# A decoder block on one core: x tile 0 by halves on a second queue, and the first head's q projected between V's k-tiles

## The chip, the core and the metric

The kernel runs on one core of a Trainium2 chip. A core has five engines with a queue of instructions each: TensorE (PE in the profile), VectorE (DVE), ScalarE (ACT), GpSimd (POOL) and SyncE (SP), which here only issues transfers. They meet through semaphores. Matrix products land in eight PSUM banks. The metric is the device time of one execution in microseconds (us), lower is better.

## The reference

One layer of a decoder block on 512 tokens of width 1024, in float32:

```python
h = rmsnorm(x, norm_attn_g[l])
u = h @ w_in[l]
u_q, u_k, u_v, u_pool, u_gate = jnp.split(u, splits, axis=-1)
a = diff_attention(q, k, v, positions, lam, subln_g[l], lam_init)   # 8 heads, rotary tables from positions
p = multiscale_pool(u_pool, w_pool[l], pool_scale[l])
merged = gates[:, :, 0] * a + gates[:, :, 1] * p
x = x + (merged @ w_out[l]).astype(x.dtype)
z = jnp.square(jax.nn.relu(rmsnorm(x, norm_mlp_g[l]) @ w_up[l]))
x = x + (z @ w_down[l]).astype(x.dtype)
return rmsnorm(x, final_norm_g)
```

## The kernel before

Every product is made of three: both factors are split into a high part (`xh`, `wh`, rounded by ScalarE) and a low part (`xl`, `wl`, the difference, by VectorE), and high x high, high x low and low x high are summed in one bank.

The program begins with the V projection. x comes transposed as eight k-tiles of 128 x 512 (`gx`, issued by SyncE at L178); `xprep` turns one into `xh` (ScalarE, L179) and `xl` (VectorE, L180), `xsquare` squares it (ScalarE, L188 and L191), and GpSimd sums the squares into `ssx` (L192). x has four buffers, so tile k+4 is fetched when tile k has been used. V has two halves of 512 columns (the loop over `n`, L203). In each, four banks take the four token tiles, and for each k-tile there are twelve matmuls of 512 columns (L221 to L223). V's weights come in tiles of two k-tiles, by halves in the first half; `split_w` casts a half (ScalarE, L112) and subtracts (VectorE, L113).

Behind V's first half `pr` (bank 4, L228) and `pc` (bank 5, L233) sum `ssx` over partitions; `rsqrt` (L195 to L201) makes the reciprocal norms `rb` and `rcol` from them on ScalarE and VectorE, and V's banks are scaled by `rcol` when they are emptied (L240, L241). V's second half has banks 4 to 7, so its token tiles 0 and 1 wait until `pr` and `pc` have been read.

VectorE works out the angles of the rotary tables meanwhile (L268 to L298), ScalarE takes their sine (L299) between two table loads, and TensorE turns the tables with eight transposes (`pt`, L311). Then the heads follow: q and k of a head are projected by 24 matmuls each (`proj`, `mm3`, L127), rotated (`rope`), and the attention is computed while products of the gates and the pool fill TensorE. `wh` and `wl` have four buffers each for all weights. Banks 0 to 2 serve projections, 3 and 4 scores, 5 and 6 transposes, 7 the heads' outputs; the warm-up matmuls at the start (L165) use bank 7 too.

The order on each engine is set at build time: a scheduler takes the program's calls in their written order as priority, replays them against a model of the engines, and writes down the order that results. A call of `after` pins two instructions. So an edit early in the program changes the order of small work far behind it.

Of the kernel before, what the change touches and what calls it, by code (L numbers as in the profile page):

```python
# [18 lines left out]
P = 128  # L19
# [32 lines left out]
def block_kernel(ctx, tc, xT, x_tok, gains, pos, consts, w_in, w_v, w_pool, w_out, w_up, w_dn, out):  # L52
    nc = tc.nc
    V, A, G, T = nc.vector, nc.scalar, nc.gpsimd, nc.tensor
    EXPLN = "natural_log_exp_and_others"
    A.preload_act_table_set(EXPLN)

    def after(later, earlier):
        tc.add_manual_dep(
# [12 lines left out]
    def bank(i, name):  # L72
        return ps.tile([P, S], F32, tag=f"b{i}", name=name)
# [13 lines left out]
    def tmp(tag, name, shape=(P, S), dt=F32, bufs=2):  # L87
        return tp.tile(list(shape), dt, tag=tag, name=name, bufs=bufs)

    def f(ap):  # L90
        return ap.bitcast(F32)
# [45 lines left out]

    con = cp.tile([P, 57], F32, name="con")
    g1c, g2c, gfc, pscc = (con[:, 8 * i : 8 * i + 8] for i in range(4))
    wv0 = load_w(w_v[0, 0], "v0_0", 2, slice(0, 1))  # L140
    nc.sync.dma_start(out=g1c, in_=consts[:, 0:8])
    invc = con[:, 32:40]
    rcc = con[:, 40:56]
    subc = con[:, 56:57]
# [26 lines left out]
    rcol = cf.tile([P, NT, 2], F32, name="rcol")  # L171
    rb = cf.tile([P, S], F32, name="rb")

    gt0 = tmp("g", "gx0", (P, 4, S), bufs=1)

    def xprep(k):
        xt = gt0[:, k % 4, :]
        nc.sync.dma_start(out=xt, in_=xT[k])  # L178
        A.activation(out=xh[:, k, :], in_=xt, func=AF.Copy, scale=g1c[:, k : k + 1])  # L179
        V.scalar_tensor_tensor(  # L180
            out=xl[k], in0=xt, scalar=g1c[:, k : k + 1], in1=f(xh)[:, k, :],
            op0=ALU.mult, op1=ALU.subtract,
        )

    def xsquare(k):
        xt = gt0[:, k % 4, :]
# [8 lines left out]
    def rsqrt(dst, src, t, n):  # L195
# [4 lines left out]
        V.scalar_tensor_tensor(out=t, in0=src, scalar=n * EPS, in1=t, op0=ALU.add, op1=ALU.mult)  # L200
        V.scalar_tensor_tensor(out=dst, in0=t, scalar=-3.0, in1=dst, op0=ALU.add, op1=ALU.mult)  # L201

    for n in range(2):  # L203
        accs = [bank(4 * n + t, f"v{n}_{t}") for t in range(NT)]
        for kk in range(4):
            if n == 0:
                xprep(2 * kk)
            if n == 0 and kk == 0:
                raw, hi, lo = wv0
                nc.sync.dma_start(out=raw[:, 512:], in_=w_v[0, 0, :, 512:])  # L210
            else:
                raw, hi, lo = load_w(w_v[n, kk], f"v{n}_{kk}", 2 if n == 0 else 1)
            for k2 in range(2):
                if n == 0 and k2 == 1:
                    xprep(2 * kk + 1)
                sl = slice(k2 * 512, k2 * 512 + 512)
                split = split_w(raw, hi, lo, sl, eng=V)
                k = 2 * kk + k2
                for t in range(NT):
                    tsl = slice(t * P, t * P + P)  # L220
                    T.matmul(accs[t], lhsT=xh[:, k, tsl], rhs=hi[:, sl], start=k == 0, stop=False)  # L221
                    T.matmul(accs[t], lhsT=xh[:, k, tsl], rhs=lo[:, sl], start=False, stop=False)
                    T.matmul(accs[t], lhsT=xl[k][:, tsl], rhs=hi[:, sl], start=False, stop=k == NK - 1)  # L223
                if n == 0:
                    after(xsquare(k), split)
        if n == 0:
            pr = bank(4, "pr")
            T.matmul(pr, lhsT=ones, rhs=ssx, start=True, stop=True)  # L228
            rsqrt(rb, pr, tmp("sq", "nt1"), D)
            A.mul(out=rb, in_=rb, mul=-0.5)  # L230
            pc = bank(5, "pc")
            for t in range(NT):
                T.matmul(pc[:, 2 * t : 2 * t + 2], lhsT=ssx[:, t * P : t * P + P], rhs=ones[:, 0:2], start=True, stop=True)  # L233
            rct = cf.tile([P, NT, 2], F32, name="rct")
            rsqrt(rcol, pc[:, 0:8].rearrange("p (a b) -> p a b", a=NT), rct, D)
            A.mul(out=rcol, in_=rcol, mul=-0.5)
        for t in range(NT):
            vd = [v_[:, 4 * n : 4 * n + 4, t * P : t * P + P] for v_ in (vh, f(vh), vl)]
            av = accs[t].rearrange("p (h d) -> p h d", h=4)
            A.activation(out=vd[0], in_=av, func=AF.Copy, scale=rcol[:, t, 0:1])  # L240
            V.scalar_tensor_tensor(  # L241
                out=vd[2], in0=av, scalar=rcol[:, t, 0:1], in1=vd[1],
                op0=ALU.mult, op1=ALU.subtract,
            )
# [57 lines left out]
    for i, fill in ((0, 1.0), (1, 0.0)):  # L302
        tk = tmp("q1", f"rt{i}", (P, NT, 2, 8, 8))
        G.memset(tk, fill)
        for c in range(2):
            for x_ in range(2):
                sc = -1.0 if (i == 1 and x_ == 0) else 1.0
                V.tensor_scalar(out=tk[:, :, c, x_, :], in0=arg[:, i], scalar1=sc, scalar2=None, op0=ALU.mult)
        pt = bank((0, 1)[i], f"pt{i}")
        for t in range(NT):  # L310
            T.transpose(out=pt[:, t * P : t * P + P], in_=tk[:, t].rearrange("p c x f -> p (c x f)"), identity=ident)  # L311
        tab = cf.tile([P, S], F32, name=f"tab{i}")
        V.tensor_tensor(out=tab, in0=pt, in1=rb, op=ALU.mult)
        tabs.append(tab)
# [31 lines left out]
    def qk(h):  # L346
        qs = tp.tile([P, 2, S], F32R, tag="qs", name=f"qs{h}", bufs=2)
        ks = tp.tile([P, 2, S], F32R, tag="ks", name=f"ks{h}", bufs=2)
        kz = kzs[h % 2]
        q = rope(proj(h, f"q{h}", V), f"q{h}")  # L350
        for c, own, oth in ((0, lo_, hi_), (1, hi_, lo_)):
            A.copy(out=qs[own, c, :], in_=q[own])
            V.tensor_tensor(out=qs[oth, c, :], in0=q[own], in1=f(qs)[own, c, :], op=ALU.subtract)
# [618 lines left out]
```

## Time and profile before

| what | us |
|---|---|
| median of 3 runs | 678.95 |
| lowest and highest | 678.44, 679.31 |
| the profiled execution, its own time | 679.05 |
| its span | 677.1 |
| TensorE busy in the span | 665.5 (98%) |
| VectorE, ScalarE, GpSimd busy | 514.8, 460.8, 170.8 |
| TensorE's granted clock | 0.997 of full speed |

A busy time is the sum over an engine's instructions; which engine sets the end at a place is read from who waits there. In a row of the timeline the brackets hold the engine's idle time before the instruction and whose work ended it. Matmuls overlap, so the distance of two starts, not the duration shown, is the cost of one.

### The profile page before, as it was taken

What the parts mean: (1) busy time and instruction counts of PE and PEld (TensorE: products, weight loads), DVE (VectorE), ACT (ScalarE), POOL (GpSimd) and SP (SyncE); (2) the same over time, 40 slices, a digit from 0 to 9 for tenths busy, and PEclk for the clock granted to TensorE, in tenths of its full rate; (3) what the DMA queues carried; (4) which work ended last, traced back from release to release, by engine and by line L of the source; (5) the groups of instructions that cost most, each with busy time, mean ns of one, the idle gap of its engine ahead of it and who ended that gap; (6) DMA issues with size and microseconds to landing.
All of it is one profiled execution on the core that took longest, in us unless ns stands there. A gap on an engine that the chain in (4) does not pass through costs nothing.

```text
span 677.1 us, 10004 instructions
## 1 busy us (share of the span) xinstructions
PE 665.5 (98%) x3686; PEld 579.0 (86%) x3686; DVE 514.8 (76%) x845; ACT 460.8 (68%) x739; POOL 170.8 (25%) x169
## 2 busy tenths in 40 slices
PE   8999999999999999999999999999999999999995
PEld 7788878887888888888889988899889998899885
DVE  6953878697878966775478999667994699747995
ACT  7554577958789687985467886367743696356874
POOL 6201543255445535520201021202103021210120
PEclk9999999999999999999999999999999999999998
DMA  8624563517163455466885589676959579493963
GB/s 272 188 97 126 136 153 106 110 66 179 48 162 109 100 140 140 91 148 228 294 217 105 162 178 259 138 190 157 236 183 200 187 162 260 124 220 126 217 125 124
DMA packets 32592, 109.34 MB, mean 161 GB/s; under 512 B 4000, under 2 KB 4640, under 8 KB 32544
## 3 DMA queue, kind: packets, MB, share of 16 engines
q0 software_dynamic: 10656, 38.80, 31.9%
q1 hardware_dynamic: 21744, 69.64, 29.0%
q8 instruction: 29, 0.48, 0.3%
q10 hardware_dynamic: 144, 0.26, 0.1%
q14 instruction: 19, 0.16, 0.1%
HBM read 106.59 MB, written 2.10 MB: 161 GB/s over the span
## 4 chain that ended last, share of the span: by engine, by line
PE 77%; DVE 8%; DMA 5%; ACT 5%; issue 4%; SPq 0%; POOL 0%; DVEq 0%; ACTq 0%; POOLq 0%
PE dm L817 7%; PE dm L819 7%; PE dm L820 7%; PE um L738 7%; PE um L743 7%; PE um L740 7%; DMA wga_uNone<-w_up 4%; PE gp L131 2%; PE gp L132 2%; PE gp L135 2%; PE k L135 2%; PE k L132 2%; PE k L131 2%; PE q L131 2%; PE q L132 2%
## 5 line engine op out<-in xcount | busy, mean ns | idle before, releaser
L649 POOL DMA_DIRECT2D wga_dNone<-w_dn x16 | 14.2, 885 | 152.2 <-DVE wl_dt L113 152.2
L819 PE MATMUL dm<-wh_dt,z 128*128 128x512 f32 (+1 forms) x128 | 49.5, 386 | 0.0
L820 PE MATMUL dm<-wl_dt,z 128*128 128x512 f32 (+1 forms) x128 | 49.4, 386 | 0.0
L817 PE MATMUL dm<-wh_dt,z 128*128 128x512 f32 (+1 forms) x128 | 49.0, 387 | 0.0
L740 PE MATMUL um<-gss,wh_ut 128*128 128x256 f32 x192 | 48.1, 283 | 0.0
L738 PE MATMUL um<-gss,wh_ut 128*128 128x256 f32 x192 | 48.0, 283 | 0.0
L649 POOL DMA_DIRECT2D wga_uNone<-w_up x18 | 15.6, 865 | 118.6 <-DVE wl_ut L113 95.5
L377 ACT ACTIVATE p<-p,st 128x128 f32<-128x128 f32 (+3 forms) x64 | 35.7, 559 | 12.4 <-DVE st L373 11.8
L835 DVE TENSOR_TENSOR x<-x,dm 128x512 f32<-128x512 f32 x48 | 32.5, 679 | 15.2 <-PE dm L820 15.2
L112 ACT CAST wh_ut<-wga_uNone 128x1024 fp32r<-128x1024 f32 x24 | 24.8, 1051 | 28.1 <-PE dm L819 19.5
L112 ACT CAST wh_ub<-wr_u 128x1024 fp32r<-128x1024 f32 x24 | 25.1, 1050 | 24.0 <-PE um L740 10.9
L113 DVE TENSOR_TENSOR wl_ub<-wr_u,wh_ub 128x1024 fp32r<-128x1024 f32 x24 | 29.1, 1219 | 12.4 <-ACT wh_ub L112 12.4
L113 DVE TENSOR_TENSOR wl_ut<-wga_uNone,wh_ut 128x1024 fp32r<-128x1024 f32 x24 | 29.0, 1221 | 11.5 <-ACT wh_ut L112 11.5
L820 PE MATMUL dm<-wl_db,z 128*128 128x512 f32 x96 | 37.2, 389 | 0.0
L819 PE MATMUL dm<-wh_db,z 128*128 128x512 f32 x96 | 37.2, 389 | 0.0
L740 PEld LDWEIGHTS um<-gss,wh_ut 128*128 128x128 f32 x192 | 36.9, 192 | 0.0
L738 PEld LDWEIGHTS um<-gss,wh_ut 128*128 128x128 f32 x192 | 36.7, 192 | 0.0
L817 PE MATMUL dm<-wh_db,z 128*128 128x512 f32 x96 | 35.8, 390 | 0.0
L714 DVE TENSOR_TENSOR z<-rawz,z 128x1024 fp32r<-128x1024 f32 x28 | 33.6, 1215 | 0.5 <-ACT z L711 0.5
L112 ACT CAST wh_dt<-wga_dNone 128x1024 fp32r<-128x1024 f32 x24 | 24.7, 1047 | 13.3 <-issue 5.1
L740 PE MATMUL um<-gab,wh_ub 128*128 128x256 f32 x128 | 32.4, 284 | 0.0
L738 PE MATMUL um<-gab,wh_ub 128*128 128x256 f32 x128 | 32.1, 283 | 0.0
(316 smaller groups left out, 2246.6 us busy)
## 6 DMA issues: line engine op xcount, KB each, us to landing
wr_u<-w_up SPq DMA_DIRECT2D x24, 512.0 KB, 5.7
wr_d<-w_dn SPq DMA_DIRECT2D x24, 512.0 KB, 4.2
wga_uNone<-w_up POOLq DMA_DIRECT2D x18, 512.0 KB, 7.1
wga_dNone<-w_dn POOLq DMA_DIRECT2D x16, 512.0 KB, 5.5
wr_q<-w_in SPq DMA_DIRECT2D x8, 512.0 KB, 3.4
wr_k<-w_in SPq DMA_DIRECT2D x8, 512.0 KB, 3.8
wr_ga<-w_in SPq DMA_DIRECT2D x8, 512.0 KB, 3.3
wr_gp<-w_in SPq DMA_DIRECT2D x8, 512.0 KB, 3.4
```

What stands on the lines that cost most here:

```text
L112: ins = A.copy(out=hi[:, sl], in_=raw[:, sl])
L113: (eng or G).tensor_tensor(out=lo[:, sl], in0=raw[:, sl], in1=f(hi)[:, sl], op=ALU.subtract)
L131: T.matmul(acc, lhsT=hi[:, c], rhs=rh[:, k, :], start=k == 0, stop=False)
L132: T.matmul(acc, lhsT=hi[:, c], rhs=rl[k], start=False, stop=False)
L377: A.activation(out=pr[:, c, :N], in_=pr[:, c, :N], func=AF.Exp, scale=-1.0, bias=st[:, c : c + 1], accum_out=st[:, 2 + c : 3 + c])
L714: V.tensor_tensor(out=z[:, 1], in0=r, in1=f(z[:, 0]), op=ALU.subtract)
L738: m = T.matmul(a_, lhsT=hi[:, c], rhs=rh[:, k, :], start=p + k == 0 and onto is None, stop=False, skip_group_check=True)
L740: T.matmul(a_, lhsT=hi[:, c], rhs=rl[:, k, :], start=False, stop=False, skip_group_check=True)
L743: m = T.matmul(a_, lhsT=lo[:, c], rhs=rh[:, k, :], start=False, stop=k == 3, skip_group_check=True)
L817: m = T.matmul(a_, lhsT=zh, rhs=hi[:, sl], start=p == 0 and start, stop=False, skip_group_check=True)
L819: T.matmul(a_, lhsT=zl, rhs=hi[:, sl], start=False, stop=False, skip_group_check=True)
L820: end = T.matmul(a_, lhsT=zh, rhs=lo[:, sl], start=False, stop=p == 3, skip_group_check=True)
```

## The change

x tile 0 is fetched by two transfers of 256 columns which ScalarE issues ahead of its first table load, and is copied and subtracted by halves. SyncE sends the gain column `con` ahead of V's first weights. The weights of head 0's q are fetched and split inside V's first half (after the second weight tile), and q is projected into bank 7 in single k-tiles: the source writes those of k-tiles 0 to 3 behind V's k-tiles 4 to 7, and the other four behind V's first half, ahead of `pr`. V's second half uses banks 4, 5, 6 and 0, and the table transposes banks 3 and 2. Head 0's attention takes its q from bank 7 instead of projecting it.

```diff
-    A.preload_act_table_set(EXPLN)
...
+    gt0 = tmp("g", "gx0", (P, 4, S), bufs=1)
+    for i in range(2):
+        nc.scalar.dma_start(out=gt0[:, 0, i * 256 : i * 256 + 256], in_=xT[0, :, i * 256 : i * 256 + 256])
+    A.preload_act_table_set(EXPLN)
+    nc.sync.dma_start(out=g1c, in_=consts[:, 0:8])
     wv0 = load_w(w_v[0, 0], "v0_0", 2, slice(0, 1))
-    nc.sync.dma_start(out=g1c, in_=consts[:, 0:8])
...
     def xprep(k):
         xt = gt0[:, k % 4, :]
-        nc.sync.dma_start(out=xt, in_=xT[k])
-        A.activation(out=xh[:, k, :], in_=xt, func=AF.Copy, scale=g1c[:, k : k + 1])
-        V.scalar_tensor_tensor(
-            out=xl[k], in0=xt, scalar=g1c[:, k : k + 1], in1=f(xh)[:, k, :],
-            op0=ALU.mult, op1=ALU.subtract,
-        )
+        if k:
+            nc.sync.dma_start(out=xt, in_=xT[k])
+        for sl in (slice(0, 512),) if k else (slice(0, 256), slice(256, 512)):
+            A.activation(out=xh[:, k, sl], in_=xt[:, sl], func=AF.Copy, scale=g1c[:, k : k + 1])
+            V.scalar_tensor_tensor(
+                out=xl[k][:, sl], in0=xt[:, sl], scalar=g1c[:, k : k + 1], in1=f(xh)[:, k, sl],
+                op0=ALU.mult, op1=ALU.subtract,
+            )
...
+    def q0_step(k):
+
+        c = slice(k * P, (k + 1) * P)
+        hi, lo = wq0[1:]
+        T.matmul(q0, lhsT=hi[:, c], rhs=xh[:, k, :], start=k == 0, stop=False)
+        T.matmul(q0, lhsT=hi[:, c], rhs=xl[k], start=False, stop=False)
+        T.matmul(q0, lhsT=lo[:, c], rhs=xh[:, k, :], start=False, stop=k == NK - 1)
+
+    q0 = bank(7, "q0")
     for n in range(2):
-        accs = [bank(4 * n + t, f"v{n}_{t}") for t in range(NT)]
+        accs = [bank((0, 1, 2, 3, 4, 5, 6, 0)[4 * n + t], f"v{n}_{t}") for t in range(NT)]
...
                 if n == 0:
                     after(xsquare(k), split)
+                    if k > 3:
+                        q0_step(k - 4)
+            if n == 0 and kk == 1:
+                wq0 = load_w(w_in[0], "q0", 2)
+            if n == 0 and 0 < kk < 3:
+                i = kk - 1
+                split_w(*wq0, slice(i * 512, i * 512 + 512), eng=V)
         if n == 0:
+            for k in range(4, NK):
+                q0_step(k)
             pr = bank(4, "pr")
...
-        pt = bank((0, 1)[i], f"pt{i}")
+        pt = bank((3, 2)[i], f"pt{i}")
...
-        q = rope(proj(h, f"q{h}", V), f"q{h}")
+        q = rope(proj(h, f"q{h}", V) if h else q0, f"q{h}")
```

The order that results is shown at three places. First SyncE at the start of the program; `wr_v` is a tile of V's raw weights, `gx` x. Before:

```order
L106 DMA wr_v_0_75<-w_v 128x512
L141 DMA con<-consts 128x8
L178 DMA gx_112<-xT 128x512
L210 DMA wr_v_0_75<-w_v 128x512
L178 DMA gx_112<-xT 128x512 x2
```

SyncE now, at the same place:

```order
L144 DMA con<-consts 128x8
L105 DMA wr_v_0_79<-w_v 128x512
L223 DMA wr_v_0_79<-w_v 128x512
L181 DMA gx_74<-xT 128x512 x2
L105 DMA wr_v_1_163<-w_v 128x512 x2
```

x tile 0 has left SyncE's queue, `con` stands first, and x tiles 1 and 2 are one place earlier. Next TensorE from the end of V's k-tile 3 to the low parts of k-tile 4 (`v_0` to `v_3` are the token tiles' banks). Before, k-tile 4 followed at once:

```order
L223 MATMUL v_3_116<-wh_v_1_162,xla 128x512
L221 MATMUL v_0_113<-wh_v_2_207,xh 128x512
L222 MATMUL v_0_113<-wl_v_2_208,xh 128x512
L221 MATMUL v_1_114<-wh_v_2_207,xh 128x512
L222 MATMUL v_1_114<-wl_v_2_208,xh 128x512
L223 MATMUL v_0_113<-wh_v_2_207,xlb 128x512
```

TensorE now: behind k-tile 3's last matmul stand six q matmuls (`q`, of x tiles 0 and 1), of which the row first shown here is the last:

```order
L213 MATMUL q_115<-xh,wl_q_209 128x512
L211 MATMUL q_115<-xh,wh_q_208 128x512
L234 MATMUL v_0_116<-wh_v_2_218,xh 128x512
L234 MATMUL v_1_117<-wh_v_2_218,xh 128x512
L234 MATMUL v_2_118<-wh_v_2_218,xh 128x512
L234 MATMUL v_3_119<-wh_v_2_218,xh 128x512
L212 MATMUL q_115<-xla,wh_q_208 128x512
L235 MATMUL v_0_116<-wl_v_2_219,xh 128x512
L236 MATMUL v_0_116<-wh_v_2_218,xlb 128x512
```

So eight q matmuls stand ahead of k-tile 4's first low part; one more of the 24 stands ahead of k-tile 7, and 15 between k-tile 7 and `pr`. Last ScalarE between the weights of V's second half (`wh_v_1` to `wh_v_3` are its tiles 1 to 3) and the norm, `arg` being the tables' angles. Before:

```order
L112 CAST wh_v_2_390<-wr_v_2_388 128x512 x2
L112 CAST wh_v_3_422<-wr_v_3_420 128x512 x2
L299 ACT_TABLE_LOAD
L299 ACTIVATE arg<-arg 128x64
L300 ACT_TABLE_LOAD
L197 ACTIVATE rb<-pr,eps 128x512
```

ScalarE now:

```order
L111 CAST wh_v_1_395<-wr_v_1_393 128x512 x2
L321 ACT_TABLE_LOAD
L321 ACTIVATE arg<-arg 128x64
L322 ACT_TABLE_LOAD
L111 CAST wh_v_2_427<-wr_v_2_425 128x512 x2
L111 CAST wh_v_3_459<-wr_v_3_457 128x512 x2
L201 ACTIVATE rb<-pr,eps 128x512
```

The sine and its two table loads stand two weight tiles earlier, and these two are cast between the second load and the norm. On TensorE, V's second half does token tile 2 alone for 24 matmuls before token tile 0, where it did tiles 2 and 3 for 36.

## Rows read from the trace of the kernel before

**Rows 1.** Stages: us, busy time (instructions) of PE, PEld, DVE, ACT, POOL, clock, DMA

```profile
5.61:29.01 23.40, 22.89 (x96) 17.82 (x97) 21.54 (x38) 16.11 (x30) 10.37 (x7) 1.00 0.75 248
29.01:53.38 24.37, 24.37 (x115) 20.03 (x114) 15.73 (x42) 15.09 (x25) 0.00 (x0) 1.00 0.40 131
```

**Rows 2.** Timeline of TensorE: start us, us, engine, line, operation

```profile
5.61 0.50 PE L221 MATMUL v<-wh_v,xh 128*128 128x512 f32 x1 [0.77 <-ACT xh L179]
...
11.29 1.07 PE L221 MATMUL v<-wh_v,xh 128*128 128x512 f32 x4
...
12.63 0.50 PE L222 MATMUL v<-wl_v,xh 128*128 128x512 f32 x1 [0.27 <-DVE wl_v L113]
...
17.97 0.39 PE L222 MATMUL v<-wl_v,xh 128*128 128x512 f32 x1
...
18.35 0.73 PE L223 MATMUL v<-wh_v,xlb 128*128 128x512 f32 x2
...
20.75 0.39 PE L221 MATMUL v<-wh_v,xh 128*128 128x512 f32 x1
...
21.37 0.50 PE L223 MATMUL v<-wh_v,xlb 128*128 128x512 f32 x1 [0.23 <-DVE xlb L180]
...
29.01 1.02 PE L228 MATMUL pr<-ssx,onesr 128*128 128x512 f32 x2
...
30.68 0.49 PE L221 MATMUL v<-wh_v,xh 128*128 128x512 f32 x1
...
52.59 1.04 PE L311 MATMUL pt<-ident,rt 128*128 128x128 f32 x8
```

**Rows 3.** Chain of waits, single issues (us to landing), casts, and 7 to 8 us

```profile
0.74 0.37 SPq L106
1.64 0.42 SPq L178
2.58 5.05 DMA gx<-xT
7.66 0.73 ACT xh L179
...
wr_v<-w_v SPq DMA_DIRECT2D x1, 256.0 KB, 2.6
...
gx<-xT SPq DMA_DIRECT2D x1, 256.0 KB, 3.1
...
3.41 0.62 ACT L112 CAST wh_v<-wr_v 128x512 fp32r<-128x512 f32 x1 [1.40 <-DMA wr_v<-w_v]
...
23.66 0.39 ACT L444 CAST wt<-wpr 128x256 fp32r<-128x256 f32 x1
...
7.00:8.00 1.00, 1.00 (x6) 0.82 (x5) 0.34 (x1) 0.97 (x2) 0.00 (x0) 1.00 1.04 395
```

**Rows 4.** Timeline of GpSimd and VectorE inside V's first half

```profile
10.71 1.32 POOL L192 TENSOR_TENSOR ssx<-ssx,sq 128x512 f32<-128x512 f32 x1 [0.39 <-ACT sq L191]
10.80 3.48 DVE L113 TENSOR_TENSOR wl_v<-wr_v,wh_v 128x512 fp32r<-128x512 f32 x2
...
15.91 0.68 DVE L113 TENSOR_TENSOR wl_v<-wr_v,wh_v 128x512 fp32r<-128x512 f32 x1
...
16.51 1.78 DVE L180 SCALAR_TENSOR_TENSOR xlb<-gx,con,xh 128x512 fp32r<-128x512 f32 x1
```

**Rows 5.** Timeline of ScalarE and VectorE from V's second half's weights to the norm

```profile
29.25 1.14 ACT L112 CAST wh_v<-wr_v 128x512 fp32r<-128x512 f32 x2 [1.49 <-PE v L223]
...
33.30 0.18 DVE L298 TENSOR_SCALAR arg<-k__476 128x32 f32<-128x32 f32 x1
...
33.79 1.28 ACT L300 ACT_TABLE_LOAD   x1
...
37.21 0.69 DVE L200 SCALAR_TENSOR_TENSOR nt<-pr,nt 128x512 f32<-128x512 f32 x1 [1.84 <-ACT nt L199]
```

**Rows 6.** Waits of TensorE from 53 to 345 us: in total, times, longest (first of three)

```profile
PE t L386 <- DVE p L382: 1.4, 1, 1.4
```

More of the change, by code (lines that the diff above doesn't have):

```diff
@@ L172, in block_kernel @@
     rb = cf.tile([P, S], F32, name="rb")
-    gt0 = tmp("g", "gx0", (P, 4, S), bufs=1)
     def xprep(k):
         xt = gt0[:, k % 4, :]
-        nc.sync.dma_start(out=xt, in_=xT[k])
-        A.activation(out=xh[:, k, :], in_=xt, func=AF.Copy, scale=g1c[:, k : k + 1])
-        V.scalar_tensor_tensor(
-            out=xl[k], in0=xt, scalar=g1c[:, k : k + 1], in1=f(xh)[:, k, :],
-            op0=ALU.mult, op1=ALU.subtract,
-        )
+        if k:
[6 more added lines that the diff above has]
+            )
     def xsquare(k):
```

## The prediction

> **What bounds the kernel now.** I read the busy time by stage first, then TensorE's own rows at the start, then the chain of waits that leads to its first matmuls, then VectorE, GpSimd and ScalarE beside them, last what TensorE waits for in the attention. The reader is to see that TensorE sets the end nearly everywhere: in the stage of V's second half it is busy 24.37 of 24.37 us, in the stage of V's first half 22.89 of 23.40 [rows 1]. What can be won is therefore what TensorE loses, and where it starts.
>
> V's two halves have 96 matmuls each. The second half runs from 30.68 to 52.59, 21.91 us, or 0.228 us each; the first runs from 5.61 to 29.01, 23.40 us [rows 2]. So the first half loses 23.40 - 21.91 = 1.49 us after its start. By start times and 0.228 a matmul [rows 2]: k-tile 2 has four matmuls from 11.29, which end at 12.20, and goes on at 12.63 (0.43, and 0.11 for the slower matmul after a wait); k-tile 4 goes on at 18.35 where 18.20 was due (0.15, and 0.10 after it); k-tile 5 at 21.37 where 20.98 was due (0.39, and 0.11). That is 0.54, 0.25 and 0.50; the 0.20 left stands at the first matmul and at k-tile 1. All three waits end on VectorE, which writes the low parts `wl` and `xl`.
>
> Why VectorE is late there: a low part takes it 0.68 us with GpSimd quiet, but the two from 10.80 take 3.48 and the one at 16.51 takes 1.78, beside GpSimd's additions to `ssx`, such as that at 10.71 for 1.32 [rows 4]. So each addition costs VectorE some 1.1 us.
>
> The first matmul at 5.61 waits for ScalarE's copy of x tile 0. That tile is SyncE's third transfer: issued at 1.64, landed 3.1 us later. The first half of V's first weight tile is issued at 0.74 and lands 2.6 us later; ScalarE casts it at 3.41, for 0.62 [rows 3]. x tile 1 lands at 2.58 + 5.05 = 7.63 and its copy ends at 8.39 [rows 3].
>
> The profiled execution took 679.05 us for a span of 677.1, so 1.95 lie around the span; the median of the runs shown is 678.95, 0.10 less. My sums start from 679.05. What a measurement can tell from no change is 0.2%, 1.36 us: faster is below 677.6, slower above 680.3.
>
> **The change part by part.** *The q projection moves.* 24 matmuls of head 0 leave the place behind the table transposes and stand in V's first half and right behind it. The work on TensorE is the same, 24 x 0.228 = 5.47 us. Unchanged in effect, V's first half with q would end at 29.01 + 5.47 = 34.48, and what counts is how much sooner it ends now.
>
> *x tile 0 by halves from ScalarE.* Its first half is issued at 0.74 instead of 1.64, and SyncE sends `con` first, so the weight half goes out at about 1.17. It lands after 2.6 to 3.1 us [rows 3], at 3.77 to 4.27; with the cast of 0.62 and some 0.1 between, the first matmul comes at 4.5 to 5.0. I take 4.6, the row nearest in kind being the same tile's own 2.6: 1.0 sooner. The table load waits behind the two issues, 2 x 0.42 as SyncE's at 1.64; it takes 1.28 [rows 5] and ends near 2.9, before the x half can be there. Were it not hidden, it would cost at most those 0.84. Two half copies in place of one: a copy of 256 columns takes 0.39 where 512 take 0.62 [rows 3], so 0.16 more, on engines that still wait for data then.
>
> Of that 1.0 us little survives: tile 0's twelve matmuls end 2.85 us after their start, near 7.45, and then k-tile 1 needs x tile 1. Its issue moves up by one slot of SyncE (2.58 to 2.05), 0.53. But the DMA engines are full there: from 7 to 8 us their share is 1.04 at 395 GB/s [rows 3], and the bytes ahead of tile 1 are the same. I take 0.43 us, near the 0.53 of the issue; bounds 0 and 1.0 (all of the start).
>
> The Trainium skill, page "DMA: Bandwidth & Descriptors", section "Issuing engines are not separate DMA queues", says that transfers issued from several engines share the same 16 DMA engines, and that only issue time is saved. By it, with the bytes ahead unchanged, the 0.43 would be 0 and the time 0.43 later; the trace's full share bears it out for bytes, but shows the issue slot as well.
>
> *The cover behind k-tile 3.* Before k-tile 4's low parts TensorE now has eight matmuls of q, 1.82 us. VectorE gets the two splits of q's weights in the same stretch: 2 x 0.6 to 0.68, say 1.26, if GpSimd is quiet, 2 x 1.74 = 3.5 if both meet an addition. ScalarE gets two casts, 2 x 0.62; its copy of a tile comes ahead of VectorE's subtraction of the same tile, so they show only if they make it the later of the two. With 1.26 TensorE's need moves back by 0.56 more than VectorE does: the 0.25 at k-tile 4 and the 0.50 at k-tile 5 are covered. With 3.5 it would lose 1.7 more instead. I take 0.75 of gain: the row at 15.91 is the quiet kind, and ScalarE's two casts also push back the square that starts GpSimd's next addition. k-tile 2's 0.54 comes before any q and stays.
>
> *The rest of q stands behind k-tile 7*, 16 matmuls without a wait, ahead of `pr`. So the reciprocal norm comes 5.47 us later against V's first half, and that is where the new wait may be (second rival). *Weights:* the 512 KB of q's weights go out earlier, ahead of V's third tile; they take 512 KB / 395 GB/s = 1.3 us of the DMA engines and shift V's later tiles, which are wanted 1.8 us later too: nothing on the path. *Banks:* V's second half has one bank fewer that is free at once, and the transposes go to banks 3 and 2, which V's first half has left by then. Behind the transposes TensorE's order is the old one less 24 matmuls; attention and MLP have the same work.
>
> Sum: 0.43 + 0.75 = 1.18 us, 679.05 - 1.18 = **677.9 us**.
>
> **The rivals.**
>
> *A better start.* x tile 1 comes as early as the issue and a second queue allow, and k-tile 2's wait shrinks with it: end of V and q near 4.6 + 0.11 + 120 x 0.228 = 32.1, 2.4 us sooner. For it: the 0.90 us between tile 0's old and new issue, of which I count half. Against it: the next rival's chain caps the gain at about 1.8, as worked out there. Time 677.2, and with some luck in the attention 676.3.
>
> *The norm's chain stops V's second half: slower.* Before, V's second half could fill two banks for 36 matmuls, 8.2 us, before it needed bank 4, which holds `pr`. Now only tile 2's bank is free: 24 matmuls. With `pr`, `pc` (29.01 to 30.68, 1.67) bank 4 is wanted 1.67 + 5.47 = 7.14 us after `pr` starts. It is free when VectorE has read `pr`, at 37.21 + 0.69 = 37.90 before, 8.89 after `pr`, and 2.83 after the second table load's end at 33.79 + 1.28 = 35.07 [rows 5]. Now two weight pairs of 1.14 are cast between that load and the norm, so it is 2.83 + 2.28 = 5.1 after it. TensorE waits from the point where the second load ends later than 7.14 - 5.1 = 2.0 us after `pr` starts. Before, it ends 6.06 after. If it keeps that distance, the price is 6.06 - 2.0 = 4.1, and the time 677.9 + 4.1 = 682. It speaks against it that the load waits for VectorE's argument of the sine, at 33.48 [rows 5], and that VectorE has as many splits ahead of that as before (22: two of q for two of V's second half). So the load stays near 35.1 less VectorE's 0.4, 34.7, while `pr` moves to 33.3: 1.4 after it, 0.6 short of the point. A `pr` at 32.7 or sooner meets it, which is the cap of 1.8.
> The Trainium skill, page "ScalarE: Activation LUTs", section "What ACT_TABLE_LOAD costs", gives 2.66 us for a switch of tables with its drain. By that the load would end 1.4 later, and 0.8 us would be lost here, 678.7; the trace has 1.28, and the next instruction stands at the end of it, so I give it no more than part of this rival's chance.
>
> *VectorE takes the cover.* Both splits of q meet additions, k-tile 4 waits 1.7 more, nothing is gained there: 679.05 - 0.43 + 1.7 = 680.3. For it: of the four low parts shown three are slow [rows 4].
>
> *The attention gives it back.* The order of the small work changes on all engines through the attention. Before, TensorE loses 2.3 us there in three waits, the longest 1.4 [rows 6]. The new order draws anew: from 0 to twice 2.3. A wait more of 1.1 to 1.4 brings the time to 679.1.
>
> **How the numbers follow.** Chances: forecast 0.45 (own range 677.3 to 678.5), better start 0.25, norm's chain 0.10, VectorE 0.08, attention 0.12. Below 677.6 lie the better start and a third of the forecast's own range: 0.40. Above 680.3 lie the chain, half of VectorE's case: 0.14. Between them 0.46. The range is 676.3 to 680.3: below it lies only a start at the floor with an attention that loses less, above it most of the chain's case.
>
> **What would show it.** In the profile after: first V matmul at 4.6, k-tile 1 at 8.0, no wait of TensorE between the first q matmul and `pr`, `pr` at 33.3; the second table load ending under 2.0 us behind it and no wait before V tile 0 of the second half; the first matmul behind the transposes near 58 us. The prediction is wrong if `pr` starts after 34.5 or TensorE waits in V's second half, or if the waits between 58 and 300 us sum to over 3.5 us.

## The result, and the profile after

The changed kernel takes 680.05 us (median of 17 runs, 677.83 to 681.3), the kernel before 678.75 (17 runs, 677.89 to 680.13). The ratio is 1.0018, with an interval of 1.0011 to 1.0025: slower by 1.2 us, where 1.1 us less was forecast. The profiled execution took 680.05 for a span of 678.2. The front, up to the tables, came out nearly as forecast, by errors that cancel; the time was lost behind it.

TensorE's timeline from V's first matmul to the first one behind the tables (columns as in [rows 2]):

```profile
4.97 2.07 PE L234 MATMUL v<-wh_v,xh 128*128 128x512 f32 x4
6.85 0.45 PE L235 MATMUL v<-wl_v,xh 128*128 128x512 f32 x1
...
8.72 1.07 PE L234 MATMUL v<-wh_v,xh 128*128 128x512 f32 x4
...
19.38 0.39 PE L212 MATMUL q<-xla,wh_q 128*128 128x512 f32 x1
19.79 0.50 PE L235 MATMUL v<-wl_v,xh 128*128 128x512 f32 x1
...
33.56 1.02 PE L250 MATMUL pr<-ssx,onesr 128*128 128x512 f32 x2
...
35.23 0.49 PE L234 MATMUL v<-wh_v,xh 128*128 128x512 f32 x1
...
57.15 1.04 PE L333 MATMUL pt<-ident,rt 128*128 128x128 f32 x8
57.94 0.48 PE L130 MATMUL q<-xh,wh_q 128*128 128x512 f32 x1
```

`pr` starts at 33.56 where 34.48 would be unchanged in effect [rows 2], and the tables at 57.15 instead of 52.59 + 5.47 = 58.06: 0.9 us are won there. The stages behind it, of before and then of after (us, busy time and instructions of PE, PEld, DVE, ACT, POOL, clock, DMA share, GB/s), begin to turn at 190 us:

```profile
57.50:95.00 37.50, 37.12 (x167) 30.23 (x167) 23.60 (x41) 20.49 (x33) 17.26 (x15) 1.00 0.56 140
95.00:190.00 95.00, 93.59 (x455) 77.90 (x454) 76.07 (x178) 75.78 (x148) 39.16 (x32) 1.00 0.44 113
190.00:300.00 110.00, 109.54 (x532) 91.65 (x531) 84.85 (x203) 90.51 (x172) 51.90 (x44) 1.00 0.50 121
```

```profile
57.50:95.00 37.50, 37.50 (x176) 31.29 (x175) 25.55 (x50) 23.76 (x37) 17.33 (x15) 1.00 0.61 147
95.00:190.00 95.00, 94.23 (x461) 78.68 (x460) 78.44 (x179) 75.93 (x148) 39.91 (x33) 1.00 0.44 114
190.00:300.00 110.00, 107.89 (x513) 88.86 (x513) 87.70 (x198) 86.77 (x169) 50.80 (x43) 1.00 0.49 116
```

TensorE loses 1.0 less up to 190 us and 1.65 more from there to 300. The waits of TensorE from 58 to 300 us of after, which answer to [rows 6] (us in total, times, longest):

```profile
PE t L408 <- DVE p L404: 1.4, 3, 0.7
PE u L130 <- DVE g L472: 1.0, 1, 1.0
PE ga L130 <- DVE g L488: 0.2, 1, 0.2
```

Of the lead at equal work nothing is left at 290 us. After TensorE has done 236, 396, 792 and 1188 units of 512 columns, before stands at 61.4, 99.5, 195.5 and 290.0 us, after at 60.5, 97.6, 193.1 and 290.3; the last matmul but one starts at 669.87 and 670.67.

Since busy time hides short stops between overlapping matmuls, I count from here on what TensorE loses by its starts: the distance of each start to the next, less the median distance for that size (0.227 us for 512 columns, 0.120 for 256, 0.108 for 128), summed over the same work. In the table "V" runs from the first warm-up product, which counts as work too, up to 236 units, so it holds the wait ahead of V's first matmul and head 0's first projections. "heads" runs to 396, "middle" to 792, "late" to 1188, "rest" to the last matmul but one; "end" is from that one's start to the end of the span (the last matmul follows 0.12 us behind it). Each row but the last column comes from one profiled execution.

| kernel | V | heads | middle | late | rest | end | ratio to before (interval) |
|---|---|---|---|---|---|---|---|
| before | 4.81 | 1.16 | 2.65 | 1.60 | 1.02 | 7.20 | 1 |
| after | 3.92 | 0.14 | 2.12 | 4.39 | 1.47 | 7.56 | 1.0018 (1.0011 to 1.0025) |
| start_alone_order_old | 4.38 | 1.19 | 2.65 | 1.60 | 0.66 | 7.31 | 0.9995 (0.9987 to 1.0004) |
| q0_alone_order_new | 5.43 | 0.14 | 2.11 | 4.43 | 0.37 | 7.25 | 1.0033 (1.0023 to 1.0042) |
| q0_alone_order_old | 8.14 | 1.23 | 2.64 | 1.60 | 1.01 | 7.27 | 1.0057 (1.0045 to 1.0069) |
| front_old_order_new | 5.62 | 0.14 | 2.13 | 4.28 | 0.72 | 7.20 | 1.0030 (1.0018 to 1.0042) |
| front_new_order_old | 7.80 | 1.57 | 2.63 | 1.62 | 1.14 | 7.55 | 1.0034 (1.0021 to 1.0047) |
| order_old_banks_right | 4.18 | 1.19 | 2.69 | 1.60 | 1.29 | 7.55 | 1.0001 (0.9990 to 1.0012) |
| order_new_then_old | 4.19 | 0.14 | 5.89 | 1.64 | 1.20 | 7.56 | 1.0011 (0.9998 to 1.0023) |
| gpsimd_order_old_there | 5.03 | 0.14 | 2.11 | 4.13 | 0.70 | 7.55 | 1.0000 (0.9989 to 1.0011) |
| order_new_then_old_2 | 4.00 | 0.14 | 2.09 | 1.58 | 0.97 | 7.55 | 0.9970 (0.9959 to 0.9982) |
| q0_low_parts_by_dma | 3.25 | 0.14 | 2.14 | 4.35 | 0.58 | 7.56 | 0.9998 (0.9989 to 1.0006) |
| before_banks_of_tables | 5.69 | 0.15 | 2.76 | 1.81 | 1.04 | 7.19 | 0.9991 (0.9982 to 1.0000) |
| after_bank4_for_table | 3.54 | 0.21 | 3.32 | 1.60 | 0.47 | 7.55 | 0.9989 (0.9979 to 0.9998) |
| late_te_new_rest_old | 4.50 | 0.14 | 2.10 | 3.93 | 0.55 | 7.57 | 1.0003 (0.9994 to 1.0012) |
| late_te_old_rest_new | 3.56 | 0.14 | 2.12 | 12.28 | 1.14 | 7.54 | 1.0156 (1.0130 to 1.0182) |
| best_of_both | 5.38 | 0.14 | 2.09 | 1.56 | 0.89 | 7.56 | 0.9979 (0.9969 to 0.9989) |

After less before, by stretch: -0.89 - 1.02 - 0.53 + 2.79 + 0.45 + 0.36 = 1.16 us, the difference of the two spans. "V" and "rest" vary from one execution to the next, "heads", "middle" and "late" hardly do where the order is the same.

Of late's 4.39 us in the changed kernel six stops of over 0.15 take 3.1; before has one such stop there, 0.62. TensorE's rows at the stops with the longest waits, of before and then of after:

```profile
269.05 0.50 PE L131 MATMUL u<-xh,wh_u 128*128 128x512 f32 x1 [0.46 <-DVE g L450]
```

```profile
218.38 0.30 PE L408 MATMUL t<-ident,p 128*128 128x128 f32 x1 [0.30 <-DVE p L404]
...
229.82 0.30 PE L408 MATMUL t<-ident,p 128*128 128x128 f32 x1 [0.39 <-DVE p L404]
...
268.89 0.50 PE L130 MATMUL u<-xh,wh_u 128*128 128x512 f32 x1 [1.03 <-DVE g L472]
...
277.23 0.50 PE L130 MATMUL ga<-xh,wh_ga 128*128 128x512 f32 x1 [0.24 <-DVE g L488]
```

### The profile page after: what moved, and what is told of

Its sections match the earlier page's. It is cut to its first block, busy times and chain, and to the rows that moved or that the text cites. A ratio compares the mean times of both kernels' runs of the same rounds, so it can differ in the third digit from the quotient of the medians.

```text
span 678.2 us, 10010 instructions
## 1 busy us (share of the span) xinstructions
PE 666.5 (98%) x3686; PEld 579.9 (85%) x3686; DVE 519.7 (77%) x847; ACT 460.2 (68%) x741; POOL 171.1 (25%) x169
## 4 chain that ended last, share of the span: by engine, by line
PE 74%; DVE 8%; ACT 7%; DMA 5%; issue 4%; POOL 1%; SPq 0%; ACTq 0%; DVEq 0%; POOLq 0%
PE dm L839 7%; PE dm L841 7%; PE dm L842 7%; PE um L760 7%; PE um L765 7%; PE um L762 7%; DMA wga_uNone<-w_up 4%; PE v L234 2%; PE v L235 2%; PE v L236 2%; PE ga L130 2%; PE ga L131 2%; PE gp L134 2%; ACT p L399 1%; PE gp L130 1%
## 5 line engine op out<-in xcount | busy, mean ns | idle before, releaser
L762 PE MATMUL um<-gab,wh_ub 128*128 128x256 f32 x128 | 32.4, 284 | 0.3 <-DVE gab L643 0.3
L733 ACT CAST z<-rawz 128x1024 fp32r<-128x1024 f32 x28 | 28.7, 1047 | 5.9 <-DVE rawz L742 4.8
```

The source lines that it names most:

```text
L762: T.matmul(a_, lhsT=hi[:, c], rhs=rl[:, k, :], start=False, stop=False, skip_group_check=True)
```

## The experiments

Most kernels here hold the order of TensorE's, VectorE's, ScalarE's and GpSimd's instructions from the first head on, as a list of places, by pins like those of the call `after`; SyncE's transfers come in the same sequence from there on in all traces. In these kernels the line numbers are some 99 to 102 higher, or L175 for every operation in four of them, where a helper records the operations. "Old" is the order of the kernel before, "new" that of the changed kernel; the change's start alone leaves the old order as it is, and q0's move alone makes the new one.

```diff
+ORDER = {"PE": "0:22 ...", "DVE": "...", "Activation": "...", "Pool": "..."}
...
+        for i, j in zip(idx, idx[1:]):
+            tc.add_manual_dep(
+                mine[j], mine[i].name,
+                mybir.DependencyInfo(mybir.DependencyClass.NoSync, mybir.DependencyReason.DATA), reason="issue order",
+            )
```

### Front and order crossed

front_new_order_old: the changed kernel with the list of the old order, and

```diff
     acc = Rot((0, 1, 2))
+    acc.n = 1
```

> The changed kernel, with every engine's instructions from the first head to the end of the program held in the order that they have in the kernel before; the front (x tile 0 by halves, q0 between V's k-tiles, banks) is the changed one. In the changed kernel pr starts 0.92 us sooner than the old V half with q's 5.47 would give (33.56 for 34.48), and what TensorE loses to waits of over 0.09 us between 58 and 300 us is 4.9 us for 3.9 before, 3.9 of it behind 170 us. Theory A (the order of the small work lost it): with the old order the gain of the front stays, pr near 33.6, the waits from 150 to 300 us back near 2.5, time 678.75 - 0.9 = 677.8, and down to 676.9 if head 0's waits at 86 and 92 us (0.9) go as in the changed kernel. Theory B (the attention has a length of its own, set by VectorE, and being early is waited out, whatever the order): the waits grow by what the front gained, 678.7 or more, up to the 680.0 of the changed kernel.

680.49 us (1.0034). Neither theory gave that, but the table decides between them: the waits of "middle" and "late" are those of before to 0.03 us, though the front is another and TensorE comes 3.4 us later. The time went at one place, on TensorE behind the tables' transposes:

```profile
57.62 1.04 PE L175 MATMUL pt<-ident,rt 128*128 128x128 f32 x8
60.60 0.47 PE L175 MATMUL q<-xh,wh_q 128*128 128x512 f32 x1 [1.94 <-DVE tab L175]
...
62.07 0.63 PE L175 MATMUL q<-xh,wh_q 128*128 128x512 f32 x1
62.50 0.63 PE L175 MATMUL q<-xla,wh_q 128*128 128x512 f32 x1
62.92 0.63 PE L175 MATMUL q<-xh,wh_q 128*128 128x512 f32 x1
```

With `acc.n = 1` q1 falls into bank 2, where the second table stands, and waits until it is read; then eight matmuls go at 0.43 us each, and from 62.1 to 65.3 us the granted clock is 0.50, the level of 1.2 GHz. That came with my choice of banks, not with the order. So, with k0 in bank 0 and q1 in bank 1 (the line above left out):

> As front_new_order_old, but the heads' projections take their banks as in the changed kernel (k0 in bank 0, q1 in 1), not one bank on. In front_new_order_old q1 stood in bank 2 and waited 2.1 us for the second table to be read out of it, and eight matmuls behind that wait were 0.43 apart instead of 0.23 (1.6 us more); its waits behind 75 us were those of the kernel before to 0.03 us. Theory A (each order brings its own waits, whatever the front): those 3.7 us go, the attention loses what it loses before, and the front's gain is all that is left: 680.5 - 3.7 = 676.8 by that run, 678.7 - 0.9 = 677.8 by the traces of before and after; I expect 677.0 to 678.0. Theory B (the attention waits out what the front gains): 678.7.

678.82 us (1.0001). The 3.7 us are gone, heads, middle and late are those of before, and by the table the front's gain stands (4.18 for 4.81). The end takes 0.35 of it, and "rest" 0.27. The time fits B's 678.7, the waits do not: they are the old order's, not grown by what the front gained. A's time, 677.0 to 678.0, did not come: by the time alone B would have won here.

front_old_order_new, the mirror: the kernel before with the list of the new order and `acc.n = 2`.

> The kernel before up to the first head, with q0 projected where it was (in bank 2), and from there every engine's instructions held in the order of the changed kernel. Theory A: the new order loses in the attention what it loses in the changed kernel, and the front's 0.92 is not there: 680.05 + 0.9 = 681.0 (680.4 to 681.9). Theory B: the order is worth nothing, TensorE comes later and waits less: 678.7 as before, to 679.3.

680.84 us (1.0030), as theory A said: heads, middle and late are 0.14, 2.13 and 4.28, the changed kernel's within 0.11. Theory B is out. The new order costs 6.55 to 6.68 us of stops where the old costs 5.41: 1.1 to 1.3 more, whatever the front.

### The two halves of the change alone

start_alone_order_old has the change's lines for `gt0`, `con` and `xprep`, and q0 as before; q0_alone_order_old and q0_alone_order_new the rest of the diff, x tile 0 as before.

> The kernel before with only its start changed: x tile 0 by halves from ScalarE's queue, con ahead of V's weights; q0 as before, the order from the first head on held as before. In the changed kernel the first V matmul came at 4.97, but four of the first five are 0.43 apart where 0.23 is usual, and k-tile 1 came at 8.72, later than before's 8.47, although its copy had ended near 7.4. Theory S1 (TensorE's slow pace there takes the start's gain): the same again, k-tile 1 at 8.7, and since x's later tiles come 1.0 sooner the wait of 0.54 at k-tile 2 goes: V's first half ends 0.3 sooner, 678.4. Theory S2 (the slow matmuls are a chance of that one execution): k-tile 1 near 7.7 to 8.0, V's first half ends 0.5 to 1.0 sooner, 677.9.

> The kernel before with only q0 moved (its weights, its steps between V's k-tiles, the banks); x tile 0 whole on SyncE's queue as before, the order behind the first head's q held as before. If q's matmuls cover k-tiles 4 and 5 as predicted, pr starts near 34.48 - 0.75 = 33.7 and the time is 678.0 with the old order (theory A), 678.7 or more by theory B. If VectorE takes the cover, pr starts at 34.5 or later, 678.8 and up.

> Only q0 moved, x tile 0 as before on SyncE's queue, and behind the first head's q the order of the changed kernel. Against front_old_order_new (680.84, the same order with the old front) this shows q's term alone: forecast 0.75, so 680.1. If the cover is worth nothing: 680.8. If the start was worth nothing in the changed kernel: as that, 680.05.

The start alone: 678.3 us, 0.9995 (0.9987 to 1.0004), in this execution three slow matmuls and `pr` 0.42 sooner (28.59): S1 by the trace; the time's interval holds S1, S2 and no change. q0 alone, in its own order: 681.09 us, 1.0033. Against front_old_order_new (1.0030) the time shows no gain by its cover. Its trace can't price the cover: slow matmuls at V's start cost 1.6 us there, and TensorE, so late, waits at neither k-tile 4 nor 5. With the old order it is slower still, 682.5, by the same wait for bank 2 as above (2.1 us at 59.92), so that run says nothing of the cover. The loss of the change belongs to q0's move, with the order that it brings.

### What takes the cover

The timeline of VectorE in the changed kernel, from q0's low parts to k-tile 4's, and that of TensorE with its wait for the last of them in order_old_banks_right, whose front is the same:

```profile
13.95 2.38 DVE L112 TENSOR_TENSOR wl_q<-wr_q,wh_q 128x512 fp32r<-128x512 f32 x2
16.25 1.79 DVE L184 SCALAR_TENSOR_TENSOR xlb<-gx,con,xh 128x512 fp32r<-128x512 f32 x1
17.96 1.77 DVE L112 TENSOR_TENSOR wl_v<-wr_v,wh_v 128x512 fp32r<-128x512 f32 x1
```

```profile
20.09 0.50 PE L334 MATMUL v<-wl_v,xh 128*128 128x512 f32 x1 [0.49 <-DVE wl_v L211]
```

```diff
-                split_w(*wq0, slice(i * 512, i * 512 + 512), eng=V)
+                raw, hi, lo = (t_[:, i * 512 : i * 512 + 512] for t_ in wq0)
+                A.copy(out=hi, in_=raw)
+                A.mul(out=lo, in_=f(hi), mul=-1.0)
+                G.dma_start(out=lo, in_=w_in[0, :, i * 512 : i * 512 + 512], accum_op=ALU.add)
```

> The changed kernel, its order from the first head on held; only the low parts of q0's weights come as those of the pool's weights do (ScalarE writes -wh, an adding transfer of GpSimd's queue puts w on it) instead of VectorE's two subtractions. In five executions of the changed front VectorE spent 2.38 to 2.39 us on the two, then 1.78 and 1.77 on xl and wl of k-tile 4 beside GpSimd's additions, and TensorE waited 0.65 to 0.77 for that wl in four of them (0.19 in the fifth), where the kernel before lost 0.25 at k-tile 4 and 0.50 at k-tile 5. Theory V (VectorE's 2.4 us for q0 take the cover): the wait at k-tile 4 goes, pr starts 0.7 to 0.9 sooner than the 33.6 to 34.7 of those five, time 679.2. Rival (ScalarE or the adding transfer is late instead, or x and its additions set the pace): the wait moves or stays, 680.0 or above.

678.8 us (0.9998), 1.4 less than the changed kernel by the ratios. The wait at k-tile 4 is gone, `pr` starts at 32.89, and late is still the new order's 4.35. Theory V holds: `pr` is 0.9 sooner than the mean of nine executions with VectorE's subtractions (33.79), as expected; about 0.3 us is lost at k-tile 5 now. The time fell by 0.4 more than expected, with 0.58 in "rest" for 1.47. VectorE's next two low parts, 1.79 and 1.77 in the changed kernel, now miss GpSimd's additions; GpSimd also issues the transfer here, at 13.93, and adds from 14.67 on, where in the changed kernel it added from 14.08, so a part of the gain may be that shift (VectorE's timeline of this kernel):

```profile
13.64 0.73 DVE L283 SCALAR_TENSOR_TENSOR xlb<-gx,con,xh 128x512 fp32r<-128x512 f32 x1
14.30 0.68 DVE L211 TENSOR_TENSOR wl_v<-wr_v,wh_v 128x512 fp32r<-128x512 f32 x1
```

### Where in the order it lies

order_new_then_old and order_new_then_old_2 are the changed kernel with lists that go over from the new order to the old one, in the first near 190 us, in the second some 8 us later.

> The changed kernel, in its own order up to some 190 us (the place where both orders have done the same work on each engine) and in the order of the kernel before from there. Up to there TensorE loses 0.6 less in the new order than in the old, behind it 2.9 more (4.2 for 1.3). Theory A: only the waits behind 190 us go, 680.05 - 2.9 = 677.2. If the late waits come from what the new order did before 190 us: 680.0.

The late waits are the old order's (1.64), but the seam itself costs 3.8 us (middle 5.89 for 2.12): TensorE waits for a gate (2.0 us) and runs slowly behind the wait (1.7), with a granted clock of 0.50 from 189.5 to 192.7 us. From its timeline:

```profile
188.88 0.51 PE L582 MATMUL pp<-dh,wt 128*128 128x512 f32 x1 [1.86 <-DVE g L571]
...
189.50 0.63 PE L586 MATMUL pp<-dh,wt 128*128 128x512 f32 x1
189.93 0.63 PE L582 MATMUL pp<-dh,wt 128*128 128x512 f32 x1
190.35 0.63 PE L585 MATMUL pp<-dl,wt 128*128 128x512 f32 x1
```

> As order_new_then_old, with the change from the new order to the old one set some 8 us later, behind both products of the pool (pp), since the seam there made TensorE wait 2.0 us for a gate and then run a dozen matmuls at 0.43 (2.1 more). In that run the waits from 215 to 270 us were those of the old order (1.35 instead of 4.19 by the distances of TensorE's starts). Theory A (each order brings its own waits, the late ones come from the order behind 190 us): without the seam 680.05 - 2.84 = 677.2, from 676.5 to 677.8. If the late waits come back, or others take their place: 679 to 680.

676.84 us, 0.9970 (0.9959 to 0.9982): faster than both kernels. Middle is the new order's 2.09, late the old one's 1.58, 2.8 less than in the changed kernel; 677.2 was expected. What TensorE waits for from 58 to 300 us there:

```profile
PE t L507 <- DVE p L503: 0.7, 1, 0.7
PE u L229 <- DVE g L571: 0.5, 1, 0.5
```

Then one place of the late part. In the changed kernel GpSimd's product of head 4's o with its gate stands behind both `ks` and the first window addition, and VectorE's merge waits for it; the two rows are from its timeline of GpSimd and VectorE:

```profile
219.46 1.29 POOL L480 TENSOR_TENSOR o<-o,g 128x512 f32<-128x512 f32 x1
220.78 1.51 DVE L489 TENSOR_TENSOR o<-o,g 128x512 f32<-128x512 f32 x1 [2.08 <-POOL o L480]
```

gpsimd_order_old_there changes seven places of GpSimd's list.

> The changed kernel in its own order on TensorE, VectorE and ScalarE; on GpSimd alone seven instructions near 213 to 225 us go back to the order of the kernel before: head 4's o times its gate (line 480) stands ahead of the second ks and of the first window addition pa, not behind both. In the changed kernel o starts at 219.46 there (214.43 before) and VectorE's merge o<-o,g waits 2.08 us for it, until 220.78 (215.74 before), with the next scores and the p that the transposes want queued behind. Theory G (that one place makes VectorE late and brings the waits of 217 to 268 us, some 2.0 of the 2.9): 678.0. Theory A in the large (the orders of all engines count, no single place): 679.5 to 680.0.

679.01 us (1.0000), which looks like theory G, but late is 4.13 for 4.39: of the 2.8 us 0.26 go. The rest of the 1.2 us by the ratios is not in this stretch ("rest" is 0.70 for 1.47 in these two executions), and I can't say that it comes from the edit. G fails by the trace.

late_te_new_rest_old and late_te_old_rest_new hold different orders behind the seam on TensorE and on the other three engines.

> The changed kernel; behind the seam near 195 us VectorE, ScalarE and GpSimd go on in the old order, TensorE stays in the new one. Late waits (190 to 300 us) by the distances of TensorE's starts: 4.2 to 4.3 in the new order, 1.4 in the old. Theory R (the order on the engines that feed TensorE brings them): near 1.4, time as order_new_then_old_2, 676.8 to 677.5. Theory T (TensorE's own order of small work brings them): near 4.2, time 679.5 to 680. A wait that comes only because the two orders don't fit would show at a new place.

> The mirror of late_te_new_rest_old: behind the seam TensorE goes on in the old order, VectorE, ScalarE and GpSimd in the new one. Theory R: late waits near 4.2, 679.5 to 680. Theory T: near 1.4, 676.8 to 677.5.

TensorE's new order beside the old one of the others still loses 3.93, as theory T says of the trace; the time, 678.82 us, is below its 679.5 to 680, with 0.55 in "rest" for 1.47. Its waits:

```profile
PE t L507 <- DVE p L503: 1.2, 2, 0.7
PE u L229 <- DVE g L571: 1.0, 1, 1.0
PE ss L528 <- POOL sql L525: 0.2, 1, 0.2
PE ga L229 <- DVE g L587: 0.2, 1, 0.2
```

The mirror settles nothing: the two orders don't fit, 12.28 us are lost, in new waits for `s`, up to 3.6. So the late loss goes with TensorE's own order of small work more than with the others', and which pieces of it do it stays open: some of the stops (at 217 and 229 us) went when the others changed, a new one came at 233, and those at 253, 268 and 277 us stayed.

### Edits that add no work

```diff
-        pt = bank((0, 1)[i], f"pt{i}")
+        pt = bank((3, 2)[i], f"pt{i}")
```

> The kernel before with one thing changed: the two table transposes stand in banks 3 and 2 as in the changed kernel, not 0 and 1. No instruction is added or taken away, no transfer moves; the order is set anew at build time, and on TensorE some 850 of 3436 places behind the first head's q hold another instruction than before. Theory A (an order brings its own waits): the waits between 75 and 300 us (before 4.7 by the distances, changed 6.1) take a third value, and the time moves with them, by 0.5 us or more either way. Rival (only the work counts): the waits stay within 0.3 of before, 678.75.

678.46 us, 0.9991 (0.9982 to 1.0000). Heads, middle and late sum to 4.72 where before has 5.41: a third value, as theory A said, and 0.7 less. The time moved by 0.6, at the edge of what it can tell.

```diff
-        pt = bank((3, 2)[i], f"pt{i}")
+        pt = bank((3, 4)[i], f"pt{i}")
```

> The changed kernel with the second table's transposes in bank 4 instead of bank 2 and nothing else changed. The order that results is close to that of the kernel before: 113 of TensorE's 3436 places differ, where the changed kernel has 697. Theory A: its waits are near the old order's, so 680.05 - 1.4 = 678.6 and as order_old_banks_right (678.8); rival: the changed kernel's late waits come with the q0 move itself and stay, 680.0.

677.92 us, 0.9989 (0.9979 to 0.9998). One bank number of the changed kernel, and late is 1.60 again; middle grows to 3.32 for 2.12, so that heads, middle and late sum to 5.13 for 6.65. This is the changed kernel's work, q0's move and all, without its loss. So the loss is not in what is moved but in the order that came with it.

> order_new_then_old_2 (676.84) with q0's low parts by ScalarE and an adding transfer, as in q0_low_parts_by_dma. If the effects add, V's part loses 3.2 to 3.3 instead of 4.0 to 4.2 and the late part 1.4, time 676.84 - 0.8 = 676.0 (675.5 to 676.5). If the cover's gain is lost again at the same waits: 676.8.

677.57 us, 0.9979 (0.9969 to 0.9989), not the 676.0 expected. Late is 1.56 and no wait is left at k-tile 4, but V loses 5.38 in the profiled execution: the first V matmul came at 5.92, and seven of the next starts lie 0.43 us apart. That the effects add is shown of the waits, not of the time.

## Why the prediction was wrong

*What failed.* "Behind the transposes TensorE's order is the old one less 24 matmuls; attention and MLP have the same work", a term of 0 in the sum. The work is the same, the order is not: on TensorE 697 of the 3436 places behind the first head's q hold another instruction, and the new order loses 1.2 us more (heads -1.0, middle -0.5, late +2.8). The rival "The attention gives it back" named the mechanism and a price of 1.1 to 1.4, but it had a chance of 0.12, as if an unlucky order were the exception. Where an edit makes the scheduler draw a new order, the term is not 0 but unknown, and its spread (3.8 to 6.7 us of stops over the orders tried, leaving out two whose halves did not fit) is larger than what was to be won.

*The sign I would have looked for did not show it.* "Waits between 58 and 300 us over 3.5" was the mark; the view of waits has 2.6 for after and 2.3 for before. It takes in idle time that an event ended, not the slower matmuls around a stop and the stops hidden by overlap. The starts at equal work show it.

*The start.* Mis-sized. Forecast 4.6 for the first matmul and 8.0 for k-tile 1; the profile has 4.97 and 8.72. In twelve executions with the new start the first matmul came at 4.84 to 5.92 (mean 5.29), in five with the old one at 5.61 to 6.11 (5.87): 0.6 and not 1.0 won, since now V's weight half is last. It is issued at 1.18 and cast at 4.30, as ScalarE's timeline shows:

```profile
3.08 0.51 ACT L183 ACTIVATE xh<-gx,con 128x256 fp32r<-128x256 f32 x1
4.30 0.62 ACT L111 CAST wh_v<-wr_v 128x512 fp32r<-128x512 f32 x1 [0.71 <-DMA wr_v<-w_v]
...
6.68 0.72 ACT L183 ACTIVATE xh<-gx,con 128x512 fp32r<-128x512 f32 x1 [0.32 <-DMA gx<-xT]
```

x tile 1's copy ends at 7.40, 0.99 sooner than before [rows 3], not 0.43: the upper bound. The rule of the Trainium skill that I weighed ("DMA: Bandwidth & Descriptors", "Issuing engines are not separate DMA queues") would have made that no gain but issue time. The trace shows more than that: x tile 1's issue moved by 0.47 (2.58 to 2.11). The shares fit that the queue's earlier start filled DMA engines that had stood partly empty (share from 2 to 3 us 0.81 before, 0.92 after; from 3 to 4 us 0.82 and 1.04). TensorE could not use it in the profiled execution, since its first matmuls went at half pace: four starts take 1.88 us (4.97 to 6.85).

*The cover.* This term, 0.75, was worth nothing in most executions. By its own rows it was too large: the need moves back by 0.56, and the delays up to k-tile 5 are 0.15 + 0.10 + 0.39 = 0.64, so some 0.2 of the 0.75 would have stayed. K-tile 5's 0.50 went as forecast, and k-tile 2's 0.54, expected to stay, went in the profiled one. But k-tile 4's wait grew: q's two low parts took 2.38 us (1.26 forecast, 3.5 the upper bound), and both low parts behind them met additions. Of nine executions with this front seven wait there 0.64 to 0.77, the profiled one 0.19, one not at all; these two had slow matmuls at the start, which brought TensorE there later. So the rival "VectorE takes the cover" was right in its mechanism, at half its price, and q0_low_parts_by_dma shows it.

*The front as a whole.* `pr` was forecast at 33.3; it came at 33.56, and between 33.15 and 34.68 in nine executions with this front (mean 33.8). With the old front it came at 29.01, 29.83 and 29.89, which is 34.5 to 35.4 with q's 5.47. So the front wins some 0.7 us against the execution that I started from and 1.3 against the mean of three. The sum of 1.18 was about right, by two errors that cancel: the start is worth more, the cover nothing.

*The norm's chain.* Out, as forecast: the second table load ends 0.56 us behind `pr`'s start (the point was 2.0), and TensorE has no wait in V's second half. The Trainium skill's page "ScalarE: Activation LUTs" ("What ACT_TABLE_LOAD costs") makes its 2.66 us of some 1.28 for the load and 1.38 for a drain; the trace agrees on the load, 1.28 again, and has no time for the drain: ScalarE's last instruction ends 0.02 us ahead of the load, and the next starts 0.01 behind it. The rows of ScalarE's and VectorE's timeline after, which answer to [rows 5]:

```profile
32.84 1.28 ACT L322 ACT_TABLE_LOAD   x1
...
38.32 0.69 DVE L204 SCALAR_TENSOR_TENSOR nt<-pr,nt 128x512 f32<-128x512 f32 x1 [1.04 <-ACT nt L203]
```

*Not in the sum at all.* The end of the program became 0.36 us longer (next section). The 0.45 of "rest" lie mostly where `um` waits for `gab` and for its weights; "rest" varies from 0.37 to 1.47 over the seventeen executions, with TensorE in the same order from `um` on, so I put it down to the execution; that is not shown.

## What to carry to other kernels

If a scheduler sets the order, cost an edit in two parts, the work that it moves and the order that it leaves behind, and give the second a spread as wide as other orders of the same kernel show. Holding the order by a list, and crossing old and new front with old and new order, separates the two; a single time can't. Before VectorE is given work under TensorE's cover, sum its queue up to the next thing that TensorE needs, at the slow price beside GpSimd.

## What was not expected of the hardware

*TensorE at half pace.* In nine of the seventeen profiled executions V's first 1 to 11 matmuls are slow, most of their starts 0.43 us apart instead of 0.23: 512 columns in 0.427 us are 1.2 a ns, the lower of TensorE's two levels (1.2 and 2.4 GHz). The view shows a granted clock of 1.00 there, but the trace holds no clock entry for that stretch, and the view counts such a stretch as full. The first entry, 1.00, begins where the pace rises: at 6.94 us in after, at 10.61 in before_banks_of_tables, at 4.63 in before, ahead of V, and between 3.98 and 10.61 over the seventeen. Ahead of V TensorE did the warm-up products from 1.14 to 4.5 or 4.9 us and then waited, from nothing up to 1.2 us. It is not a matter of the kernel: before had no slow matmul, before_banks_of_tables, with the same front up to there, had eleven, which brought k-tile 1 2.4 us later (10.85 for 8.47) and `pr` 0.9 (29.89 for 29.01). Its timeline of TensorE:

```profile
5.75 0.80 PE L221 MATMUL v<-wh_v,xh 128*128 128x512 f32 x1 [0.83 <-ACT xh L179]
6.34 0.63 PE L222 MATMUL v<-wl_v,xh 128*128 128x512 f32 x1
6.76 0.63 PE L221 MATMUL v<-wh_v,xh 128*128 128x512 f32 x1
...
10.85 0.39 PE L221 MATMUL v<-wh_v,xh 128*128 128x512 f32 x1
```

Later in the program it came behind waits of 1.9 us (the rows at 62 and 189 us above), there with a granted clock of 0.50, and 1.6 and 1.7 us were lost after the wait itself; behind a like wait in q0_alone_order_old it did not come (1.00 from 60 to 64 us). What decides it was not tried. It adds to the scatter of this kernel's times; how much of that it makes, one profile a kernel does not show.

*The end of the program.* SyncE waits at the end for the last transfers, one semaphore after the other. Before and then after, by its waits from 670 us on:

```profile
SPq L968 <- DMA out<-x: 2.0, 2, 1.3
```

```profile
SPq L990 <- DMA out<-x: 2.3, 1, 2.3
```

In the records of before, the transfer that lands last is the last but one that SyncE waits for, and the others have been passed meanwhile. In after its semaphore has another number and is third in the row, and seven more waits of 0.06 us follow: 7.56 us from the last matmul but one to the end instead of 7.20. Kernels with both parts of the change have 7.54 to 7.57, with the start alone 7.31, with q0 alone 7.25 and 7.27, with neither 7.19 and 7.20. No wait was added to the program; the numbering alone moved.
